# Gathered copies of queries and keys for the levels of a gated recurrence, and squares moved behind the output products

## The chip, the cores and the metric

The kernel runs on one core of a Trainium2 chip. The metric is the device time of one execution in microseconds (us); a comparison is made between medians of several executions on the same chip. The engines that matter here are TensorE (PE; its weight loads are PEld in the profile), VectorE (DVE), ScalarE (ACT) and the DMA queues of SyncE (SP) and ScalarE. GpSimd (POOL) only makes masks at the start.

## The reference

One decoder layer over 2048 positions of width 1024, in float32: a norm, a mixer with two head groups side by side, an output projection, a gated MLP with a short causal convolution, a final norm. The change lies in the first head group, four heads of a gated recurrence (key and value width 128):

```python
def hgrn2_chunkwise(q, k, v, log_f):
    """S_t = diag(f_t) S_{t-1} + k_t v_t^T,  o_t = S_t^T q_t  (k_t = 1 - f_t)."""
    ...
        b = jnp.cumsum(gi, axis=2)
        rel = b[:, :, :, None, :] - b[:, :, None, :, :]
        decay = jnp.exp(jnp.where(causal, rel, -jnp.inf))
        scores = jnp.einsum('bhtk,bhsk,bhtsk->bhts', qi, ki, decay)
        intra = jnp.einsum('bhts,bhsv->bhtv', scores, vi)
        inter = jnp.einsum('bhtk,bhkv->bhtv', qi * jnp.exp(b), state)
...
        o_hg = hgrn2_chunkwise(q_hg, k_hg, v_hg, log_f)
        o_hg = rmsnorm(o_hg, hg_norm_w[l]).reshape(B, S, HG_VAL_WIDTH)
        o_hg = (o_hg * jax.nn.silu(hg.astype(jnp.float32))).astype(h.dtype)
        ...
        mix = jnp.concatenate([o_hg, o_att], axis=-1)
        h = h + mix @ w_out[l]
```

The second head group is sliding-window attention (eight heads, four pairs `j` in the kernel).

## The kernel before, in words

The sequence is handled in two halves of 1024 positions. Each half has a mixer stage (the loop over `h` = 0 to 3, where a recurrence head and an attention pair run side by side), the output projection, and the MLP. Large matrices are multiplied as three products of high and low parts (`unit`, L212, for all projections: `f`, `hq`, `q`, `g`, and `pop` for the output projection). Features lie on the 128 partitions, positions along the free axis.

The recurrence doesn't compute decays pairwise. A chunk of 128 positions is cut by halving: at level m (1, 2, 4, ... 64), blocks of 2m positions have a left half whose keys and a right half whose queries meet. `Q` holds queries scaled by the decay from the block's start, `K` keys scaled by the decay to the block's end; `F` holds the decay over each block. At each level:

- the products of left keys and right queries go to a PSUM bank `pl` (`plev` in the profile);
- right queries are multiplied with the left block's decay (L609), left keys with the right block's (L610), and `F` is merged (L616, L620);
- the valid blocks of `pl` are put into the score tile `ST`.

How the products are formed depends on level and head. For m below 32 in heads 0 to 2 (`pairs`, `place_pairs`), ScalarE copies the left keys of two neighbouring chunks into `KK` (L566), and one product of 128 keys by 128 queries covers both chunks (L569, four products a level). Half of the result belongs to the one chunk and is copied under a mask (L585); the other half lies m partitions too low: ScalarE copies it out (`moved`, L576), a DMA on ScalarE's queue shifts it (`odd`, L579), and a masked copy places it after the next level's scaling (L588). In head 3, m below 32, each chunk has a product of its own with all 128 keys and 64 queries (L602, eight a level), and one masked copy places all (L625). Levels 32 and 64 use products of m by m in parts of the array (L607) and copies (L630).

After the levels, `K` is transposed (`pkn`, L640), states are updated (`pu`, L647; `SS`, L651), and for each of eight chunks two output products are made: scores by values (L665) and queries by state (L666), in two banks `po` of four chunks each. ScalarE squares each chunk's output right behind its products (L667) for the norm; then a root by iteration (`rsqrt`), the scaling (`on`, L674), a transpose (`pot`, L679) and the gate (L680).

The four `hg` and `at` banks of PSUM are shared out in turn: `pdiag`, `plev`, `pkn`, `pu`, `po` and `pot` all take one of two `hg` banks. The order of each engine's instructions is fixed when the program is built, by a planner that goes by its own estimates of durations and by the order in which the code names the work; `issue_after` adds that one instruction comes behind another. While head 3 runs, TensorE can fill in with the output projection, `pop`, for its first three tiles (`BEHIND` holds some of these back behind `pu`, `po` and `pot` of head 3), as far as the mixed heads exist; the tiles of attention pair 3 and of recurrence head 3 come last in the order [0, 4, 1, 5, 2, 6, 7, 3].

Of the kernel before, what the change touches and what calls it, by code (L numbers as in the profile page):

```python
# [17 lines left out]
P = 128  # L18
# [25 lines left out]
KB = 2  # L44
# [6 lines left out]
def hymba_layer(ctx: ExitStack, tc: tile.TileContext, a: dict, out: bass.AP):  # L51
# [468 lines left out]
    def hgrn(hf, h, X, invb, vs, WG, mix, p, fu=None):  # L520
# [12 lines left out]
        K = p.tile([P, HALF], F32, tag="K", name="K", bufs=1)  # L533
        nc.vector.tensor_scalar(K, f, -1.0, 1.0, op0=ALU.mult, op1=ALU.add)
        Q = p.tile([P, HALF], F32, tag="Q", name="Q", bufs=1)
# [24 lines left out]
        F, left = f, None  # L560

        def pairs():


            KK = p.tile([P, HALF // 2], F32, tag="KK", name="KK", bufs=KB)
            nc.scalar.copy(KK.rearrange("p (r b c m) -> p r c b m", r=TT // 2, c=2, m=m),  # L566
                           K.rearrange("p (r c b w m) -> p r c b w m", c=2, b=nbc, w=2, m=m)[:, :, :, :, 0])
            for r in range(TT // 2):
                marks[m] = nc.tensor.matmul(pl[:, r * P:(r + 1) * P], KK[:, r * P:(r + 1) * P],  # L569
                                            Qv[:, 2 * r * nbc:2 * (r + 1) * nbc, 1], start=True, stop=True)  # L570

        def place_pairs():

            plv = pl.rearrange("p (r c t) -> p r c t", r=TT // 2, c=2)
            moved, odd = [p.tile([P, TT // 2, 64], F32, tag="lv", name=n, bufs=LV) for n in ("moved", "odd")]
            nc.scalar.copy(moved, plv[:, :, 1])  # L576

            rows_ = P - max(m, 2)
            nc.scalar.dma_start(odd[0:rows_], moved[m:m + rows_])  # L579
            if m == 1:  # L580
                nc.scalar.dma_start(odd[rows_:rows_ + 1], moved[P - 1:P])
            STv = ST.rearrange("p (r c) (b w m) -> p r c b w m", c=2, w=2, m=m)
            mk = C.lmask[m].bitcast(U32).rearrange("p (b m) -> p b m", m=m)
            mk = mk.unsqueeze(1).to_broadcast([P, TT // 2, nbc, m])
            nc.vector.copy_predicated(STv[:, :, 0, :, 1], mk, plv[:, :, 0].rearrange("p r (b m) -> p r b m", m=m))  # L585
            r = slice(0, P - m)
            ov = odd[r].rearrange("p r (b m) -> p r b m", m=m)
            return lambda: nc.vector.copy_predicated(STv[r, :, 1, :, 1], mk[r], ov)  # L588

        for m in LEVELS:  # L590
            nb = HALF // (2 * m)
            nbc = 64 // m
            Qv = Q.rearrange("p (b w m) -> p b w m", w=2, m=m)
            Kv = K.rearrange("p (b w m) -> p b w m", w=2, m=m)
            Fv = F.rearrange("p (b w) -> p b w", w=2)
            pl = ps("hg", "plev")
            paired = m < 32 and h < HG - 1
            if paired:
                pairs()
            elif m < 32:  # L600
                for c in range(TT):
                    marks[m] = nc.tensor.matmul(pl[:, c * 64:(c + 1) * 64], K[:, c * P:(c + 1) * P],  # L602
                                                Qv[:, c * nbc:(c + 1) * nbc, 1], start=True, stop=True)
            else:
                for c in range(TT):
                    for s0 in range(0, P, 2 * m):
                        nc.tensor.matmul(pl[s0:s0 + m, c * m:(c + 1) * m], K[:, c * P + s0:c * P + s0 + m],  # L607
                                         Q[:, c * P + s0 + m:c * P + s0 + 2 * m], start=True, stop=True)
            nc.vector.tensor_tensor(Qv[:, :, 1], Qv[:, :, 1], Fv[:, :, 0:1].to_broadcast([P, nb, m]), op=ALU.mult)  # L609
            done = nc.vector.tensor_tensor(Kv[:, :, 0], Kv[:, :, 0], Fv[:, :, 1:2].to_broadcast([P, nb, m]), op=ALU.mult)  # L610
# [10 lines left out]
            if paired:  # L621
                left = place_pairs()
            elif m < 32:
                mk = C.lmask[m].bitcast(U32).rearrange("p (b m) -> p b m", m=m)
                nc.vector.copy_predicated(ST.rearrange("p c (b w m) -> p c b w m", w=2, m=m)[:, :, :, 1],  # L625
                                          mk.unsqueeze(1).to_broadcast([P, TT, nbc, m]),
                                          pl.rearrange("p (c b m) -> p c b m", c=TT, m=m))
            else:
                for s0 in range(0, P, 2 * m):
                    nc.scalar.copy(ST[s0:s0 + m, :, s0 + m:s0 + 2 * m],  # L630
                                   pl[s0:s0 + m, 0:TT * m].rearrange("p (c m) -> p c m", c=TT))
        yield
# [28 lines left out]
        for c in range(TT):  # L661
            cs = slice(c * P, (c + 1) * P)
            prev = state[:, h] if c == 0 else SS[:, c - 1]
            o = po[c // 4][:, c % 4 * P:(c % 4 + 1) * P]
            nc.tensor.matmul(o, ST[:, c], v[:, c], start=True, stop=False)  # L665
            marks["po"] = nc.tensor.matmul(o, Q[:, cs], prev, start=False, stop=True)  # L666
            nc.scalar.activation(on[:, c], o, AF.Square, accum_out=ss[:, c:c + 1])  # L667
# [626 lines left out]
```

## Time and profile before

| | |
|---|---|
| three executions | 2197.66, 2198.23, 2200.65 us (median 2198.23) |
| profiled execution, span from first to last instruction | 2198.0 us (the profile gives no other time for it) |
| mean granted TensorE clock | 0.997 |
| products on TensorE, weight loads | 11424 each |
| mixer stage, head 3 | about 342 to 407 us in the first half, 1432 to 1497 us in the second |

The profile gives, for one execution, the busy time of each engine, the chain of work that ended last, groups of instructions by line, waits, and windows of time. A product's busy time holds its way through the array, and so overlaps with the next one; how fast products really follow each other is read from the chain, where each piece counts only until the next begins.

### The profile page before, as it was taken

The page shows a single profiled execution, that of the slowest core. Times are in us where ns is not written, and L with a number is a line of the kernel's source. Part 1 is how long each engine was busy: PE and PEld are TensorE (multiplying, and loading weights), DVE is VectorE, ACT ScalarE, POOL GpSimd, SP SyncE. Part 2 cuts the span into 40 slices and gives each one's busy share as a digit, 9 for nine tenths or more (in the row PEclk, how much of TensorE's full clock was granted, in tenths as well). Part 3 has the DMA queues.
Part 4 walks back from the last instruction along what each step waited for, and adds up shares of the span by engine and source line. Part 5 has one row for each costly group of instructions (what it writes and reads, how often), then busy time and mean ns, then how long its engine had stood idle before and what let it go on. Part 6 is the DMA issues. An engine that isn't in the chain of part 4 may idle for free.

```text
span 2198.0 us, 29524 instructions
## 1 busy us (share of the span) xinstructions
PE 2180.4 (99%) x11424; PEld 1834.0 (83%) x11424; DVE 1639.5 (75%) x2451; ACT 1049.9 (48%) x1848; POOL 6.3 (0%) x28
## 2 busy tenths in 40 slices
PE   9999999999999999999999999999999999999998
PEld 7988988888888888888889889888888888888888
DVE  6567568688887888885855666677888878887766
ACT  6445544454444445335735455544644444443353
POOL 1000000000000000000000000000000000000000
PEclk9999999999999999999999999999999999999999
DMA  4101112323333234964631111114132323259643
GB/s 155 51 32 48 39 41 68 119 74 102 104 109 108 89 127 143 372 241 156 209 125 41 44 36 51 58 39 134 58 125 92 125 91 109 98 183 393 233 144 130
DMA packets 94358, 257.91 MB, mean 117 GB/s; under 512 B 11594, under 2 KB 17546, under 8 KB 94218
## 3 DMA queue, kind: packets, MB, share of 16 engines
q1 hardware_dynamic: 88992, 251.30, 33.9%
q10 hardware_dynamic: 5226, 4.73, 0.7%
q8 instruction: 89, 1.46, 0.3%
q14 instruction: 51, 0.42, 0.1%
HBM read 195.10 MB, written 57.15 MB: 115 GB/s over the span
## 4 chain that ended last, share of the span: by engine, by line
PE 95%; DVE 3%; ACT 1%; DMA 1%; issue 0%; SPq 0%; DVEq 0%; ACTq 0%
PE X L877 7%; PE X L878 7%; PE X L879 7%; PE pop L212 7%; PE hq L212 4%; PE q L212 4%; PE f L212 4%; PE g L212 4%; PE Y L879 4%; PE Y L878 4%; PE Y L877 4%; PE pdx L1088 3%; PE pdx L1089 3%; PE pdx L1090 3%; PE pdy L1089 3%; PE pdy L1088 3%
## 5 line engine op out<-in xcount | busy, mean ns | idle before, releaser
L706 ACT CAST whi<-raw 128x1024 fp32r<-128x1024 f32 x88 | 92.6, 1053 | 109.2 <-PE X L878 68.2
L877 PE MATMUL X<-T,whi 128*128 128x512 f32 x352 | 136.9, 389 | 0.0
L878 PE MATMUL X<-T,whi 128*128 128x512 f32 x352 | 136.9, 389 | 0.0
L879 PE MATMUL X<-T,wlo 128*128 128x512 f32 x352 | 136.9, 389 | 0.0
L972 DVE SCALAR_TENSOR_TENSOR y<-ga,cw,y 128x1024 f32<-128x1024 f32 x88 | 112.5, 1281 | 26.0 <-ACT y L970 26.0
L884 ACT COPY u<-X 128x512 f32<-128x512 f32 x88 | 51.4, 585 | 133.3 <-PE X L879 133.1
L707 DVE TENSOR_TENSOR wlo<-raw,whi 128x1024 fp32r<-128x1024 f32 x88 | 107.3, 1220 | 0.0
L190 ACT CAST whi<-raw 128x1024 fp32r<-128x1024 f32 x57 | 59.5, 1048 | 93.1 <-PE q L212 31.9
L707 DVE TENSOR_TENSOR xld<-raw,xhd 128x1024 fp32r<-128x1024 f32 x72 | 80.8, 1133 | 19.1 <-ACT xhd L706 18.9
L706 ACT CAST xhd<-raw 128x1024 fp32r<-128x1024 f32 x72 | 69.7, 978 | 43.6 <-DMA raw<-act0T 14.8
L212 PE MATMUL pop<-XL,whi 128*128 128x512 f32 x256 | 86.1, 396 | 2.1 <-DVE XL L224 2.1
L212 PE MATMUL pop<-XH,wlo 128*128 128x512 f32 x256 | 85.2, 393 | 0.8 <-DVE wlo L191 0.8
L212 PE MATMUL pop<-XH,whi 128*128 128x512 f32 x256 | 84.5, 397 | 0.2
L878 PEld LDWEIGHTS X<-T,whi 128*128 128x128 f32 x352 | 66.1, 188 | 13.7
L877 PEld LDWEIGHTS X<-T,whi 128*128 128x128 f32 x352 | 66.1, 188 | 13.7
L879 PEld LDWEIGHTS X<-T,wlo 128*128 128x128 f32 x352 | 66.1, 188 | 13.7
L1088 PE MATMUL pdx<-xhd,hid 128*128 128x512 f32 x192 | 74.4, 391 | 1.0 <-ACT hid L706 1.0
L1089 PE MATMUL pdx<-xld,hid 128*128 128x512 f32 x192 | 74.7, 389 | 0.0
L1090 PE MATMUL pdx<-xhd,lod 128*128 128x512 f32 x192 | 73.7, 389 | 0.0
L698 PE MATMUL pvv<-whi,XH 128*128 128x256 f32 x256 | 73.5, 288 | 0.0
L191 DVE TENSOR_TENSOR wlo<-raw,whi 128x1024 fp32r<-128x1024 f32 x57 | 69.5, 1222 | 4.2 <-ACT whi L190 4.1
L699 PE MATMUL pvv<-whi,XL 128*128 128x256 f32 x256 | 72.6, 284 | 0.0
(379 smaller groups left out, 6563.3 us busy)
## 6 DMA issues: line engine op xcount, KB each, us to landing
wr<-in_w_down SPq DMA_DIRECT2D x90, 512.0 KB, 4.8
raw<-in_w_gate SPq DMA_DIRECT2D x44, 512.0 KB, 3.6
raw<-in_w_up SPq DMA_DIRECT2D x44, 512.0 KB, 3.6
raw<-act0T SPq DMA_DIRECT2D x20, 512.0 KB, 6.1
raw<-act1T SPq DMA_DIRECT2D x20, 512.0 KB, 10.1
act0B<-y SPq DMA_DIRECT2D x33, 256.0 KB, 2.6
act1B<-y SPq DMA_DIRECT2D x33, 256.0 KB, 2.4
raw<-in_w_out SPq DMA_DIRECT2D x16, 512.0 KB, 4.7
```

Of the source, the lines that this page charges most:

```text
L212: marks["unit"] = nc.tensor.matmul(o[b], w, x[:, bs], start=f, stop=l)
L698: nc.tensor.matmul(o[:, 0:256], xh[:, t], hi[:, c], start=kt == 0, stop=False)
L699: nc.tensor.matmul(o[:, 0:256], xl[:, t], hi[:, c], start=False, stop=False)
L706: return (nc.scalar.copy(h, src), (eng or nc.vector).tensor_tensor(l, src, h.bitcast(F32), op=ALU.subtract))
L707: (eng or nc.vector).tensor_tensor(l, src, h.bitcast(F32), op=ALU.subtract))
L877: nc.tensor.matmul(o, wh[:, ws], xh, start=i == 0 and not more, stop=False, skip_group_check=more)
L878: nc.tensor.matmul(o, wh[:, ws], xl, start=False, stop=False, skip_group_check=more)
L879: r = nc.tensor.matmul(o, wl[:, ws], xh, start=False, stop=i == 3, skip_group_check=more)
L972: nc.vector.scalar_tensor_tensor(y, g[:, w:w + HALF], C.cw[:, ft, w:w + 1], y, op0=ALU.mult, op1=ALU.add)
L1088: nc.tensor.matmul(o, wh[:, i, c], ah[:, i, cols], start=f, stop=False, skip_group_check=more)
L1089: nc.tensor.matmul(o, wh[:, i, c], al[:, i, cols], start=False, stop=False, skip_group_check=more)
L1090: nc.tensor.matmul(o, wl[:, i, c], ah[:, i, cols], start=False, stop=l, skip_group_check=more)
```

## The change

- `Q` and `K` become the two halves of one tile, `QK`.
- At every level of every head ScalarE copies the right queries and the left keys, 512 elements of each, into a new tile `G` (two buffers). The column order puts chunk c beside chunk c + 4, block by block.
- The products read `G`, not `Q` and `K`. Below 32 and at 64 there are four products of 128 by 128 in every head; level 32 keeps sixteen small ones.
- Queries and keys are scaled by one DVE instruction of 2 x 512 elements.
- `place` serves every head below level 32: first half from PSUM under the mask, second half by `moved`, DMA and masked copy. Its chunk pairs are c and c + 4, and it reads `pl` with blocks of m apart. Level 64 is copied to `ST` in two parts.
- All eight squares of a head are named behind its last output product.
- The SBUF reserved for DMA descriptors is set to 256 bytes a partition.

```diff
-KB = 2
+GB = 2
...
-        K = p.tile([P, HALF], F32, tag="K", name="K", bufs=1)
+        QK = p.tile([P, 2, HALF], F32, tag="QK", name="QK", bufs=1)
+        Q, K = QK[:, 0], QK[:, 1]
         nc.vector.tensor_scalar(K, f, -1.0, 1.0, op0=ALU.mult, op1=ALU.add)
-        Q = p.tile([P, HALF], F32, tag="Q", name="Q", bufs=1)
         nc.vector.tensor_tensor(Q, q, f, op=ALU.mult)
...
+        R = TT // 2
+        def place(m, pl):
+            plv = pl.rearrange("p (r b c m) -> p r b c m", r=R, c=2, m=m)
+            moved, odd = [p.tile([P, R, 64], F32, tag="lv", name=n, bufs=LV) for n in ("moved", "odd")]
+            nc.scalar.copy(moved.rearrange("p r (b m) -> p r b m", m=m), plv[:, :, :, 1])
...
+            STv = ST.rearrange("p (c r) (b w m) -> p c r b w m", c=2, w=2, m=m)
...
+            nc.vector.copy_predicated(STv[:, 0, :, :, 1], mk, plv[:, :, :, 0])
...
+            return lambda: nc.vector.copy_predicated(STv[r, 1, :, :, 1], mk[r], ov)

         for m in LEVELS:
...
+            part, step = QK.ap[0], QK.ap[-1][0]
+            own = bass.AP(QK.tensor, QK.offset + m * step, [part, [(HALF - m) * step, 2], [2 * m * step, nb], [step, m]])
+            far = bass.AP(QK.tensor, QK.offset + m * step, [part, [(HALF - m) * step, 2], [2 * m * step, nb // 2],
+                                                           [R * P * step, 2], [step, m]])
+            G = p.tile([P, 2, HALF // 2], F32, tag="G", name="G", bufs=GB)
+            nc.scalar.copy(G.rearrange("p t (b c m) -> p t b c m", c=2, m=m), far)
             pl = ps("hg", "plev")
...
+            if m == 32:
                 for c in range(TT):
+                    for b in range(2):
+                        x = slice(c % R * P + b * 64 + c // R * m, c % R * P + b * 64 + c // R * m + m)
+                        nc.tensor.matmul(pl[2 * b * m:2 * b * m + m, c * m:(c + 1) * m], G[:, 1, x], G[:, 0, x],
+                                         start=True, stop=True)
             else:
...
+                for r in range(R):
+                    x = slice(r * P, (r + 1) * P)
+                    marks[m] = nc.tensor.matmul(pl[:, x], G[:, 1, x], G[:, 0, x], start=True, stop=True)
-            nc.vector.tensor_tensor(Qv[:, :, 1], Qv[:, :, 1], Fv[:, :, 0:1].to_broadcast([P, nb, m]), op=ALU.mult)
-            done = nc.vector.tensor_tensor(Kv[:, :, 0], Kv[:, :, 0], Fv[:, :, 1:2].to_broadcast([P, nb, m]), op=ALU.mult)
+            done = nc.vector.tensor_tensor(own, own, Fv.rearrange("p b w -> p w b").unsqueeze(3).to_broadcast([P, 2, nb, m]),
+                                           op=ALU.mult)
...
+            if m < 32:
+                left = place(m, pl)
...
+                for c in range(2):
+                    nc.scalar.copy(ST[0:m, c * R:(c + 1) * R, m:],
+                                   pl[c * m:(c + 1) * m].rearrange("p (r c m) -> p r c m", c=2, m=m)[:, :, c])
...
             marks["po"] = nc.tensor.matmul(o, Q[:, cs], prev, start=False, stop=True)
-            nc.scalar.activation(on[:, c], o, AF.Square, accum_out=ss[:, c:c + 1])
+        for c in range(TT):
+            nc.scalar.activation(on[:, c], po[c // 4][:, c % 4 * P:(c % 4 + 1) * P], AF.Square,
+                                 accum_out=ss[:, c:c + 1])
...
-    nc = bacc.Bacc("TRN2", target_bir_lowering=False, num_devices=1)
+    nc = bacc.Bacc("TRN2", target_bir_lowering=False, num_devices=1, dynamic_dma_scratch_size=256)
```

More of the change, by code (lines that the diff above doesn't have):

```diff
@@ L560, in hgrn @@
         F, left = f, None
[L562 to L576, printed above, removed]
+        R = TT // 2
[3 more added lines that the diff above has]
+            nc.scalar.copy(moved.rearrange("p r (b m) -> p r b m", m=m), plv[:, :, :, 1])
             rows_ = P - max(m, 2)
@@ L581, in place_pairs @@
                 nc.scalar.dma_start(odd[rows_:rows_ + 1], moved[P - 1:P])
[L582 removed]
+            STv = ST.rearrange("p (c r) (b w m) -> p c r b w m", c=2, w=2, m=m)
             mk = C.lmask[m].bitcast(U32).rearrange("p (b m) -> p b m", m=m)
[L584 to L585 removed]
+            mk = mk.unsqueeze(1).to_broadcast([P, R, 64 // m, m])
+            nc.vector.copy_predicated(STv[:, 0, :, :, 1], mk, plv[:, :, :, 0])
             r = slice(0, P - m)
             ov = odd[r].rearrange("p r (b m) -> p r b m", m=m)
[L588 removed]
+            return lambda: nc.vector.copy_predicated(STv[r, 1, :, :, 1], mk[r], ov)
         for m in LEVELS:
@@ L596, in hgrn @@
+            G = p.tile([P, 2, HALF // 2], F32, tag="G", name="G", bufs=GB)
+            nc.scalar.copy(G.rearrange("p t (b c m) -> p t b c m", c=2, m=m), far)
             pl = ps("hg", "plev")
[L597 to L600, printed above, removed]
+            if m == 32:
                 for c in range(TT):
-                    marks[m] = nc.tensor.matmul(pl[:, c * 64:(c + 1) * 64], K[:, c * P:(c + 1) * P],
-                                                Qv[:, c * nbc:(c + 1) * nbc, 1], start=True, stop=True)
-            else:
[L605 to L608, printed above, removed]
@@ L620, in hgrn @@
                 nc.vector.tensor_tensor(F, Fv[:, :, 0], Fv[:, :, 1], op=ALU.mult)
[L621 to L628, printed above, removed]
+            if m < 32:
+                left = place(m, pl)
+            elif m == 32:
                 for s0 in range(0, P, 2 * m):
@@ L631, in hgrn @@
                                    pl[s0:s0 + m, 0:TT * m].rearrange("p (c m) -> p c m", c=TT))
+            else:
+                for c in range(2):
+                    nc.scalar.copy(ST[0:m, c * R:(c + 1) * R, m:],
+                                   pl[c * m:(c + 1) * m].rearrange("p (r c m) -> p r c m", c=2, m=m)[:, :, c])
         yield
```

2 lines of the change are left out of this document (removed).

## The prediction, made before the changed kernel ran

> **What bounds the kernel now.** I read the busy times first, then the chain that ended last, then windows over the stages, then groups by line, and last the order of single instructions in two places. The first two rows are the busy times and the chain by engine; the others are pieces of the chain in order of time (start, length, what).
>
> ```profile
> PE 2180.4 (99%) x11424; PEld 1834.0 (83%) x11424; DVE 1639.5 (75%) x2451; ACT 1049.9 (48%) x1848; POOL 6.3 (0%) x28
> ...
> PE 95%; DVE 3%; ACT 1%; DMA 1%; issue 0%; SPq 0%; DVEq 0%; ACTq 0%
> ```
> ```profile
> 57.54 10.88 PE q L212 x48
> ```
> ```profile
> 356.55 1.75 PE plev L602 x16
> ```
> ```profile
> 173.69 0.89 PE plev L569 x8
> ...
> 200.30 1.08 PE plev L607 x16
> ```
>
> TensorE carries 95% of the chain. A "busy" PE need not be a full PE, so I check its pace: 48 products of 512 columns in 10.88 us are 0.227 us each, one after the other without a hole. Where PE is fed like that, every microsecond of TensorE work that disappears shortens the kernel, and work on the other engines is free.
>
> A rule speaks against this. The Trainium skill, page "Perfetto Trace Analysis", section "Identifying the Most-Contended Engine", says that matmul busy time is a poor measure of how near TensorE is to its limit and that the busy share of the weight loads is one of the better ones. Here that share is 83%; by that reading TensorE has room, shorter TensorE work would fall into it, and the time would stay near 2196 (rival B has the same result). The even 0.227 us speaks for PE as the bound in most of the program, but not where it starves.
>
> Where does it starve? Windows of the busy times (core 0: PE, PEld, DVE, ACT, POOL, then granted clock); last, the same stretch for the general projection line L212 alone.
>
> ```profile
> 298.00:342.00 44.00, 44.00 (x253) 36.96 (x252) 24.22 (x45) 20.27 (x41) 0.00 (x0) 1.00 0.23 73
> 342.00:407.00 65.00, 62.34 (x433) 51.91 (x432) 50.61 (x100) 25.81 (x78) 0.00 (x0) 0.97 0.16 47
> ...
> 1432.00:1497.00 65.00, 62.52 (x440) 52.42 (x439) 50.44 (x101) 26.57 (x78) 0.00 (x0) 0.97 0.16 48
> ```
> ```profile
> 351.00:364.00 13.00, 13.00 (x76) 11.33 (x76) 12.31 (x26) 8.24 (x36) 0.00 (x0) 1.00 0.17 55
> 364.00:381.00 17.00, 16.32 (x169) 13.41 (x169) 14.76 (x29) 2.48 (x5) 0.00 (x0) 0.90 0.00 1
> ```
> ```profile
> 364.00:381.00 17.00, 3.28 (x11) 1.82 (x12) 0.90 0.00 1
> ```
>
> 342 to 407 and 1432 to 1497 hold head 3 of each half. PE idles 65 - 62.34 = 2.66 and 65 - 62.52 = 2.48 us there, 5.1 together, and at a clock of 0.97 the two windows lose about 2 x 65 x 0.03 = 3.9 us more. DVE is full (12.31 of 13, 14.76 of 17), and the filling products have almost run out (11 in 17 us). So head 3 is limited by DVE's recursion, with PE nearly full beside it. In the 44 us before, DVE works 24.22: there is room, if head 3 could begin earlier.
>
> What keeps it from that? Two loops in which PE is one of the steps. Here are chain pieces around head 2's output products; then DVE and PE rows of head 1's recursion (start, length); then head 3's first products.
>
> ```profile
> 305.85 0.22 PE po L665 x2
> ...
> 310.55 0.22 PE po L666 x2
> 310.77 4.36 PE q L212 x19
> 315.13 0.22 PE po L665 x2
> ...
> 326.23 0.22 PE po L666 x2
> ```
> ```profile
> 162.51 0.69 DVE L609 TENSOR_TENSOR Q<-Q,f 128x512 f32<-128x512 f32 x1 [3.94 <-PE plev L569]
> ...
> 168.68 0.69 DVE L609 TENSOR_TENSOR Q<-Q,f 128x512 f32<-128x512 f32 x1 [0.22 <-PE plev L569]
> ```
> ```profile
> 167.57 1.07 PE L569 MATMUL plev<-Q,KK 128*128 128x128 f32 x8
> 173.52 1.05 PE L569 MATMUL plev<-Q,KK 128*128 128x128 f32 x8
> ```
> ```profile
> 344.31 1.16 PE L544 MATMUL pdiag<-hg,K 128*128 128x128 f32 x8 [0.35 <-DVE hg L680]
> ```
>
> Each time PE has to wait for another engine's answer, the fixed order puts some 19 other products in between: 4.36 us after a square (310.77 to 315.13), and 167.57 - (162.51 + 0.69) = 4.4 us from a scaling of Q to the next level's products. A level therefore takes 173.52 - 167.57 = 6 us, and eight pairs of output products, 16 x 0.22 = 3.5 us of work, take 326.45 - 305.85 = 20.6 us. Head 3's first products then wait for L680, the end of head 2.
>
> **The change part by part.** Groups by line (engine, operation, shapes, count | busy us, mean ns of one | idle before), then who waited for the squares:
>
> ```profile
> L536 DVE TENSOR_TENSOR Q<-hg,f 128x1024 f32<-128x1024 f32 x8 | 9.8, 1220 | 8.3 <-PE po L666 8.3
> L609 DVE TENSOR_TENSOR Q<-Q,f 128x512 f32<-128x512 f32 x56 | 38.6, 690 | 30.9 <-PE plev L569 18.6 <-PE plev L607 11.8 <-PE plev L602 0.4
> L625 DVE COPY_PREDICATED ST<-lmask,plev 128x512 f32<-128x512 uint32 x10 | 9.5, 949 | 0.0
> L585 DVE COPY_PREDICATED ST<-lmask,plev 128x256 f32<-128x256 uint32 x30 | 16.6, 554 | 3.4 <-ACT moved L576 3.3
> L588 DVE COPY_PREDICATED ST<-lmask,odd 126x256 f32<-126x256 uint32 x6 | 4.4, 737 | 4.1 <-DMA odd<-moved 4.1
> L588 DVE COPY_PREDICATED ST<-lmask,odd 124x256 f32<-124x256 uint32 x6 | 2.6, 442 | 7.8 <-DMA odd<-moved 7.8
> ```
> ```profile
> L706 ACT CAST whi<-raw 128x1024 fp32r<-128x1024 f32 x88 | 92.6, 1053 | 109.2 <-PE X L878 68.2 <-issue 19.1 <-PE Z L878 13.8
> L566 ACT COPY KK<-K 128x512 f32<-128x512 f32 x30 | 19.1, 636 | 29.6 <-DVE K L610 21.2 <-DVE K L534 8.2
> L706 ACT CAST T<-h 128x512 fp32r<-128x512 f32 x22 | 12.8, 617 | 3.2 <-PE pop L212 3.2
> L576 ACT COPY moved<-plev 128x256 f32<-128x256 f32 x30 | 11.1, 371 | 23.8 <-PE plev L569 23.4
> L667 ACT ACTIVATE on<-po 128x128 f32<-128x128 f32 x64 | 17.6, 275 | 58.3 <-PE po L666 56.9
> L667 ACT ACTIVATION_READ_ACCUMULATOR on<-po 128x1 f32 x64 | 12.5, 195 | 0.0
> ```
> ```profile
>   PEld po L665: 1.3, 6
> ```
> ```profile
> 1450.71 3.20 ACT sc L481 x16
> ```
>
> Chunk pairs in head 3. Levels 1 to 16 of that head now use eight products of 64 columns (L602: 16 records, 1.75 us); they become four of 128 columns, as the other heads have (L569: 8 records, 0.89). Five levels, two halves: 10 x (1.75 - 0.89) = **8.6 us less TensorE work**. Placing them costs DVE L585 and L588 where it had L625: about 2 x 0.56 against 0.95, +0.17 a level; ScalarE a copy of 0.37 and its queue one issue more (two at level 1), 12 DMAs in all. In the heads that have them DVE waits for these transfers (4.1 us over six at level 2, 7.8 over six at level 4), 0.7 to 1.3 us a level, between other work.
>
> Level 64. Eight products of 64 columns (1.08 us) become four of 128 (taken as 0.89): 8 heads x 0.19 = **1.5 us less**. Its one copy out of PSUM becomes two, about +0.15 us of ScalarE each time. Level 32 keeps sixteen small products: nothing.
>
> Gathering. Seven copies of 1024 elements a head, 56 x 1.05 = 59 us of ScalarE, replace 30 x 0.636 = 19 us; with moved and level 64 that is +45 us on an engine with 1049.9 of 2198.0. Cover: ScalarE is idle half of each window above. If the cover fails, a gather stands in order behind a block of exponentials, 3.20 us (rival C). The pattern hops: at level 1 each element comes from another place than the one before. No row has that read; KK, which strides, costs 0.636 against 0.617 for a dense one of that size, and L588 with runs of two costs 0.737 against 0.442 with runs of four. So a level-1 or level-2 gather costs between 1.05 and 1.05 x 0.737/0.442 = 1.75 us; I take 1.1, since KK is the same engine. The Trainium skill, page "SBUF — State Buffer", section "Specifications (TRN2)", says that each access that crosses to a new 16-byte line pays, unless a line is hit at least twice. KK's small excess hardly agrees, L588's does; by it the level-1 gather would stand near the upper end, 0.7 us more in each head, and in the sum that is hidden all the same.
>
> One scaling. Two of 0.69 become one of 1.22: 0.16 us less DVE a level. With the placing, head 3's DVE sum stays the same.
>
> What the scaling waits for. Before: PE's products of that level. After: only the gather, so the recursion is gather 1.05 + scaling 1.22 + two hand-overs, about 2.4 us, and PE only follows; with two G buffers and two banks, one trip of 4.4 us covers two levels, so I expect 3 us a level in place of 6: some 20 us a head.
>
> Squares last. PE no longer waits for squares of the same bank (1.3 us in all), and eight pairs can run without trips: the products end up to 16 us sooner. Against it: a square of 0.275 + 0.195 us could begin after one pair of products, 0.44 us, and now begins after the four pairs of its bank, 1.76. So in head 3, where they alternate closely, the chain may end up to 1.3 us later; I take nothing, since the later products of `pop` are there to fill PE, and keep 2.6 for the range.
>
> Q and K in one tile. K for the next head now waits for the previous head's last output product, as Q already does (L536 idles 8.3 us for it). Since that product comes sooner, cost nothing; without that, up to 1.05 us for the first gather on each head's chain.
>
> Smaller DMA scratch. It makes room for G. It changes no instruction; nothing either way.
>
> **The sum.** In heads 0 to 2 PE is full, so shorter loops give nothing by themselves; they let head 2 end and head 3 begin up to 20 us earlier, into the stretch where DVE has room, with the projections still there to fill PE. Then PE is the bound throughout and its work counts: -8.6 - 1.5 = -10.1. Of the 5.1 us idle in head 3 I take half, -2.6 (bounds: 0, and 5.1 + 3.9 for idle and clock). All else is hidden. 2198.0 - 10.1 - 2.6 = **2185.3**. The sum is made on the profiled execution, span 2198.0; I put the time around the span at nothing, since the median of the runs is 2198.23, 0.2 above.
>
> **The rivals.** B, head 3 stays bound by DVE (its DVE work is the same, and 12.31 of 13 and 14.76 of 17 us of DVE were in use). Then the 8.6 us become PE idle time, and level 64 of the other heads (6 x 0.19 = 1.1) and a microsecond of bank waits remain: about 2196. For it: DVE full from 351 to 364. Against: that is so because head 3 comes late.
>
> C, slower: gathers queue behind exponentials. Place: attention's softmax of head 3, two blocks of 3.20 us per half. If head 3 is the chain and both blocks delay a gather, 2 x 2 x 3.2 = 12.8, less 2.1 of B: about 2209. It decides once the wait passes 3.3 us a half (6.5 in all less 2.1 is 0.2%). Against: ScalarE is idle 39 of 65 us there.
>
> D, all idle time and the clock recover: 2198.0 - 10.1 - 5.1 - 3.9 = 2179. For it: head 3 earlier by 20 us, more than the PE shortage. Against: attention's own chain in head 3 doesn't shorten.
>
> **Chances.** Forecast 0.50 (2181 to 2190), B 0.22, C 0.12, D 0.16. Over 0.2% is 4.4 us, about what a measurement here can tell from no change: forecast and D are faster, 0.66; B is the same, 0.22; C slower, 0.12. To hold 8 in 10 the range takes D and B in: 2178 to 2197.
>
> **What the profile after would show.** L569-like products in head 3, 0.89 us a level, and level 64 the same; 56 gathers near 1.05 us, level 1 apart; levels some 3 us apart in heads 0 to 2; output products of a head within 5 us, not 20; head 3's first products well before 342 us; PE idle in head 3 under 3 us and a clock nearer 1.00. Wrong it would be if PE idle in head 3 grew by what its work shrank (B), or if a gather there began late behind L481 (C).

## The result, and the profile after

The changed kernel takes 2182.84 us (median of four executions, 2182.57 to 2183.7) where the kernel before takes 2197.94 on the same chip (2197.41 to 2200.65): a ratio of 0.9931, 95% interval 0.9917 to 0.9945, so 15.1 us less. Its profiled execution has a span of 2182.0 us, 16.0 under that of before. Line numbers from here on are those of the changed kernel: gather L590, products L601 (level 32: L596), scaling L602, copies of levels 32 and 64 L618 and L622, key transposes L632, output products L657 and L658.

First the busy times; then the same TensorE products before and after: all level products (`plev`) over the whole span, and the output projection (`pop`) beside head 3 and behind it (window, PE busy and count, clock, DMA share, GB/s; the first three rows are of the kernel before, the last three of the changed one).

```profile
PE 2163.2 (99%) x11280; PEld 1824.8 (84%) x11280; DVE 1629.6 (75%) x2405; ACT 1095.3 (50%) x1896; POOL 6.4 (0%) x28
```
```profile
0.00:2198.00 2198.00, 65.77 (x784) 1.00 0.35 117
...
342.00:407.00 65.00, 32.83 (x129) 0.97 0.16 47
407.00:490.00 83.00, 52.56 (x232) 1.00 0.33 110
```
```profile
0.00:2182.00 2182.00, 55.94 (x640) 1.00 0.35 119
...
322.00:390.00 68.00, 26.20 (x106) 0.97 0.24 72
390.00:490.00 100.00, 63.20 (x279) 1.00 0.32 106
```

The 16.0 us divide so. The level products need 65.77 - 55.94 = 9.8 us less. TensorE's other busy time falls by 2180.4 - 2163.2 - 9.8 = 7.4. Its idle time, span less busy, rises by 1.2 (2198.0 - 2180.4 = 17.6 to 18.8). 5.1 of the 7.4 is the unchanged `pop` (183.88 to 178.81 over the span, 768 products in both): behind head 3 a product costs 0.227 us in both kernels (52.56/232, 63.20/279); beside head 3 it cost 32.83/129 = 0.254 and now costs 0.247, and fewer of them stand there (106, not 129). These parts are rough, since the busy times of neighbouring products overlap. Counted in both traces from each product's start to the next one's, the level products give 11.2 us (55.7 to 44.5) and `pop` 4.6 (180.5 to 176.0). Part of the rest is the granted clock and not the change: the profiled execution of the kernel before has one more stretch of low clock (mean 0.66 from 1108 to 1113 us, some 1.7 us lost, on products that are the same in both).

Next, the recursion's scaling in head 2, first and last of its seven levels; the gathers of its levels 1, 2, 4 and 8 with what each waited for; and the groups of both.

```profile
233.82 1.22 DVE L602 TENSOR_TENSOR QK<-QK,f 128x1024 f32<-128x1024 f32 x1
...
251.74 1.22 DVE L602 TENSOR_TENSOR QK<-QK,f 128x1024 f32<-128x1024 f32 x1
```
```profile
221.01 1.51 ACT L590 COPY G<-QK 128x1024 f32<-128x1024 f32 x1 [3.50 <-DVE QK L536]
235.07 1.17 ACT L590 COPY G<-QK 128x1024 f32<-128x1024 f32 x1 [0.26 <-DVE QK L602]
240.12 1.05 ACT L590 COPY G<-QK 128x1024 f32<-128x1024 f32 x1 [1.67 <-DVE f L609]
243.14 1.05 ACT L590 COPY G<-QK 128x1024 f32<-128x1024 f32 x1 [1.19 <-DVE QK L602]
```
```profile
L602 DVE TENSOR_TENSOR QK<-QK,f 128x1024 f32<-128x1024 f32 x56 | 68.6, 1226 | 6.0 <-ACT G L590 5.1
L590 ACT COPY G<-QK 128x1024 f32<-128x1024 f32 x56 | 63.6, 1136 | 58.9 <-DVE QK L602 29.1 <-DVE QK L536 24.1 <-DVE f L609 3.1
```

Seven levels stand 251.74 - 233.82 = 17.9 us apart from first to last, 3.0 a level where it was 6. The scaling no longer names a product among its waits; 5.1 us for the gather are left of 30.9 us for products. The gather itself costs 1.5 us at level 1 and 1.17 at level 2, and 1.05 above.

The output products of head 2, first and last (the rows between them left out), and the span of the diagonal products and of head 3's transposes (`pdiag` begins a head, `pot` ends it; the last starts are those of head 3 in the second half).

```profile
277.70 0.38 PE L657 MATMUL po<-v,ST 128*128 128x128 f32 x2
...
281.99 0.38 PE L658 MATMUL po<-SS,QK 128*128 128x128 f32 x2
```
```profile
L544 PE MATMUL pdiag<-hg,QK x128: 270/275/275, 68.2 to 1405.9; 128*128 128x128 f32 x128
...
L673 PE MATMUL pot<-ident,on x64: 270/272/329, 130.6 to 1467.7; 128*128 128x128 f32 x64
```

They take 4.7 us, not 20.6. Head 3 of the second half begins at 1405.9, where it began at 1434.8; some 8 of these 29 us are the first half's own gain.

Last, head 3: windows with the 24 us in front of it; then the rows of ScalarE and TensorE around a new wait, in both halves.

```profile
298.00:322.00 24.00, 24.00 (x129) 19.44 (x128) 9.62 (x13) 6.16 (x7) 0.00 (x0) 1.00 0.15 45
322.00:390.00 68.00, 64.18 (x427) 54.71 (x426) 55.54 (x103) 43.42 (x105) 0.00 (x0) 0.97 0.24 72
...
1405.00:1470.00 65.00, 61.93 (x420) 53.56 (x419) 54.42 (x102) 42.46 (x105) 0.00 (x0) 0.97 0.24 75
```
```profile
361.56 0.40 ACT L481 ACTIVATE sc<-sc,m 128x128 f32<-128x128 f32 x1 [0.55 <-DVE m L477]
...
365.04 0.74 ACT L622 COPY ST<-plev 64x256 f32<-64x256 f32 x2
```
```profile
365.83 1.11 PE L632 MATMUL pkn<-ident,QK 128*128 128x128 f32 x4 [2.86 <-ACT ST L622]
...
1446.36 0.66 PE L632 MATMUL pkn<-ident,QK 128*128 128x128 f32 x4 [2.44 <-ACT ST L622]
```

TensorE still idles there: 68 - 64.18 = 3.8 us and 65 - 61.93 = 3.1, and the granted clock is 0.97 as before. 5.3 of these 6.9 us are one wait, twice: the second bank of key transposes needs the PSUM bank that holds the level-64 products; L622 empties it, and stands on ScalarE behind attention's block of exponentials, 361.56 to 364.8.

The clock of 0.97 is a mean. It is full in most of head 3 and low in one stretch of each half, behind this wait (columns as in the windows above):

```profile
362.00:366.00 4.00, 1.14 (x8) 0.91 (x9) 1.19 (x4) 3.94 (x19) 0.00 (x0) 0.94 0.00 0
366.00:370.00 4.00, 4.00 (x24) 3.83 (x25) 3.25 (x5) 1.25 (x3) 0.00 (x0) 0.63 0.00 0
370.00:374.00 4.00, 3.42 (x39) 2.62 (x38) 3.89 (x13) 1.55 (x8) 0.00 (x0) 1.00 0.00 0
```

By this the stretch loses some 4 x 0.06 + 4 x 0.37 = 1.7 us, an estimate. The kernel before has one such stretch in each half too. In its second half, eight `pop` products stood 0.427 us apart there, from 1439.8 to 1443.3, so some of the slow `pop` is clock, which now falls on other products.

### The profile page after: what moved, and what is told of

Same layout as the page of the kernel before. It is cut to its first block, busy times and chain, and to the rows that moved or that the text cites. A ratio compares the mean times of both kernels' runs of the same rounds, so it can differ in the third digit from the quotient of the medians.

```text
span 2182.0 us, 29301 instructions
## 1 busy us (share of the span) xinstructions
PE 2163.2 (99%) x11280; PEld 1824.8 (84%) x11280; DVE 1629.6 (75%) x2405; ACT 1095.3 (50%) x1896; POOL 6.4 (0%) x28
## 5 line engine op out<-in xcount | busy, mean ns | idle before, releaser
L590 ACT COPY G<-QK 128x1024 f32<-128x1024 f32 x56 | 63.6, 1136 | 58.9 <-DVE QK L602 29.1
```

## The experiments

Medians in us; ratio to the kernel before on the same chip, with its 95% interval; then the clock loss (below); then from the profiled execution the span less PE busy, and where head 3 of the second half begins and ends (last starts of `pdiag` and `pot`).

| kernel | median | ratio | clock loss | PE idle | head 3 |
|---|---|---|---|---|---|
| before | 2197.9 | | 3.5 | 17.6 | 1434.8 to 1487.0 |
| changed | 2182.8 | 0.9931 [0.9917, 0.9945] | 4.4 | 18.8 | 1405.9 to 1467.7 |
| e1 | 2198.2 | 0.9999 [0.999, 1.0008] | 5.0 | 25.4 | 1430.4 to 1481.6 |
| e2 | 2202.3 | 1.0021 [1.0012, 1.0029] | 7.4 | 24.7 | 1415.9 to 1488.6 |
| e3 | 2195.5 | 0.9989 [0.998, 0.9998] | 8.4 | 23.1 | 1412.3 to 1481.7 |
| e4 | 2192.1 | 0.997 [0.9958, 0.9981] | 4.4 | 20.8 | 1410.2 to 1477.3 |
| e5 | 2182.7 | 0.9931 [0.9918, 0.9943] | 4.8 | 20.5 | 1405.6 to 1468.3 |
| e6 | 2206.6 | 1.0039 [1.0025, 1.0052] | 7.5 | 29.4 | 1424.2 to 1492.9 |
| e7 | 2190.8 | 0.9967 [0.9955, 0.998] | 5.7 | 22.9 | 1410.5 to 1476.7 |
| e8 | 2194.1 | 0.9982 [0.9973, 0.999] | 9.2 | 24.9 | 1412.3 to 1481.0 |
| e9 | 2179.6 | 0.9911 [0.9897, 0.9924] | 1.6 | 18.2 | 1403.0 to 1462.6 |
| e10 | 2181.1 | 0.9918 [0.9904, 0.9931] | 2.6 | 18.1 | 1405.2 to 1465.1 |
| e11 | 2178.7 | 0.9909 [0.9896, 0.9923] | 3.3 | 16.7 | 1403.2 to 1463.6 |
| e12 | 2180.4 | 0.9918 [0.9905, 0.9932] | 2.6 | 17.1 | 1404.3 to 1464.6 |

The clock loss is an estimate: for every execution on record, span x (1 - mean granted clock), and the mean of these. The clock is listed to 0.001, which is 2.2 us of one execution, so a mean is good to about half a us. The kernel before shows what it is worth: its executions at 0.997 took 2201.3 us on average (4 of 61), those at 0.999 took 2197.7 (26 of 61). In e2, e3, e6 and e8 the loss is 3 to 5 us above that of the kernel each is made from, in e9 to e12 it is 1 to 3 below. In the profiled executions most stretches of low clock follow a wait of TensorE, but not every wait has one (e1's of 2.59 us has none), and what sets them was not tested.

Two cautions. The spans of profiled executions lie up to 2.8 us under their kernel's median and e1's 5.5, so rows of different kernels are compared for what waits on what, not for a few us of span; and the kernel before had medians from 2197.7 to 2199.2 in the four groups of runs, so the ratio is the better measure of small differences. And the planner orders every kernel anew: e5, e9, e10 and e11 keep the order of the changed kernel's TensorE products almost everywhere, the other runs less, and e6 least, so a difference of 2 or 3 us in those can be the plan's.

The first four runs set three theories against each other: T1, TensorE's saved work counts only once head 3 begins earlier, so both halves of the change are needed; T2, TensorE is the bound anyway and its work counts by itself; T3, the loops without TensorE give the gain.

**e1: chunk pairs in head 3 alone** (the kernel before, with the smaller DMA scratch).

```diff
-            paired = m < 32 and h < HG - 1
+            paired = m < 32
```

> The kernel before, with chunk pairs in head 3 as in the other heads (TensorE work of its levels 8.6 us less), and nothing else of the change. Theory 1 (both parts are needed: shorter TensorE work counts only once head 3 begins earlier, since head 3 is otherwise limited by VectorE's recursion): 2194 to 2198 us, TensorE idle in head 3 grows by about what its work shrinks. Theory 2 (TensorE is the bound anyway): 8.6 us less, 2189. Theory 3 (the gain comes from the loops without TensorE alone): no change, 2198.

2198.2: nothing, although the 8.6 us of products are gone. TensorE waits instead; the row is its longest wait in head 3, for the low part of the projection's input.

```profile
1436.00 0.74 PE L212 MATMUL pop<-XL,whi 128*128 128x512 f32 x2 [2.59 <-DVE XL L224]
```

T2 falls. TensorE's idle time grew by 7.8 us. This is what rival B of the prediction had described, and for this part alone it holds.

**e2: squares behind the products alone** (the kernel before).

```diff
-            nc.scalar.activation(on[:, c], o, AF.Square, accum_out=ss[:, c:c + 1])
+        for c in range(TT):
+            nc.scalar.activation(on[:, c], po[c // 4][:, c % 4 * P:(c % 4 + 1) * P], AF.Square,
+                                 accum_out=ss[:, c:c + 1])
```

> The kernel before, with all squares of a head behind its last output product, and nothing else. Theory 1: the output products of heads 0 to 2 run within 5 us in place of 20, so head 3 begins up to 15 us earlier and fills better: 2 to 4 us less, 2194 to 2196. Theory 2: only TensorE's waits for a square's bank go, about 1 us: 2197. Theory 3: if the output products are the loop that mattered most, most of the 15 us: 2185 to 2190.

2202.3, by the ratio some 4 us more than before: slower, which no theory had. The larger clock loss (7.4 against 3.5) is about as much as the whole difference. Head 3 begins 19 us sooner (1415.9) and ends 1.6 later. Its first scaling comes only 17 us after the head's first products (324.6 to 341.6 in the first half), from the first scaling to the last it takes 33.6 us (28.3 before), and TensorE waits late in the head; two such waits in each half, here those of the second:

```profile
1460.61 0.40 PE L506 MATMUL poT<-po,V 128*64 128x128 f32 x2 [1.19 <-DVE m L474]
...
1467.22 0.73 PE L212 MATMUL pop<-XH,whi 128*128 128x512 f32 x2 [2.76 <-ACT XH L516]
```

An earlier begin of head 3's products is worth nothing here, where its recursion still waits for TensorE level by level.

**e3: both together**, the kernel before with e1's and e2's edits.

> The kernel before, with chunk pairs in head 3 and the squares last, without the gathered copies (and with the small DMA scratch). Theory 1: the squares let head 3 begin earlier and a part of the 8.6 us counts: 2188 to 2193. Theory 2: 8.6 and 1 us less, 2188. Theory 3 (gathering is what brought the gain): 2195 to 2198.

2195.5, by the ratio some 2 us less than before: T1's form of "both are needed" is too weak. From here to the changed kernel is the gather (with the one scaling, and level 64 for 1.5 us): 2195.5 - 2182.8 = 12.7 us, most of the whole (up to 4.0 of it the difference in clock loss).

**e4: the changed kernel with the TensorE work put back.** Head 3's products below level 32 are cut in halves of 64 queries.

```diff
+                    n = 64 if m < 32 and h == HG - 1 else P
+                    for s in range(r * P, (r + 1) * P, n):
-                    marks[m] = nc.tensor.matmul(pl[:, x], G[:, 1, x], G[:, 0, x], start=True, stop=True)
+                        marks[m] = nc.tensor.matmul(pl[:, s:s + n], G[:, 1, x], G[:, 0, s:s + n], start=True, stop=True)
```

> The changed kernel, with head 3's products below level 32 cut into halves of 64 queries, eight a level, so that TensorE's work there is again 1.75 us a level and all else stays. The result is the same. Theories 1 and 2: 8.6 us more, 2191 to 2192. Theory 3 (TensorE has room in head 3, the loops decide): 2183 to 2185.

2192.1: 9.3 us more (8.5 by the ratios), at the same clock loss, for 64.50 - 55.94 = 8.6 us more of level products (e4's whole-span sum is 64.50). The same work that e1 removed for nothing now has its full price. So T1 stands in this form: with the gather, TensorE's work in head 3 counts.

**e5: the new wait taken away.** Level 64's copies by VectorE in head 3.

```diff
-                    nc.scalar.copy(ST[0:m, c * R:(c + 1) * R, m:],
+                    (nc.vector.tensor_copy if h == HG - 1 else nc.scalar.copy)(ST[0:m, c * R:(c + 1) * R, m:],
```

> The changed kernel, with head 3's two copies of the level-64 products out of PSUM given to VectorE, so that they no longer stand behind a 3.2 us block of exponentials on ScalarE. Theory W (that wait is what holds PE for 3.02 and 2.60 us ahead of the second bank of key transposes, and nothing stands behind it): both stalls go and the time falls by 4 to 6 us, to 2177 to 2179. Rival (head 3 is held by VectorE's recursion or by attention's own chain; the wait is only where the shortage shows): the idle time of TensorE moves to other products of head 3 and the time stays at 2181 to 2184.

2182.7, no change. The wait for L622 is gone and others hold what it held: the state updates wait for the copies of the transposed keys, attention's transposes for the scaled exponentials.

```profile
366.74 2.05 PE L639 MATMUL pu<-v,Kn 128*128 128x128 f32 x16 [2.03 <-ACT Kn L633]
370.72 0.41 PE L506 MATMUL poT<-po,V 128*64 128x128 f32 x2 [1.05 <-DVE pp L498]
...
1447.41 0.68 PE L495 MATMUL ppt<-ident,sc 128*128 128x128 f32 x4 [3.48 <-DVE sc L486]
```

The rival holds: the largest wait in the profile was where a shortage showed, not what caused it.

**e6: the loop through TensorE put back.** Gather, shapes and scaling stay; the products of levels 1 to 16 and 64 read the queries where the scaling writes them.

```diff
-                    marks[m] = nc.tensor.matmul(pl[:, x], G[:, 1, x], G[:, 0, x], start=True, stop=True)
+                    q_far = bass.AP(QK.tensor, QK.offset + (r * P + m) * step,
+                                    [part, [2 * m * step, nbc], [R * P * step, 2], [step, m]])
+                    marks[m] = nc.tensor.matmul(pl[:, x], G[:, 1, x], q_far, start=True, stop=True)
```

> The changed kernel, but the products of levels 1 to 16 and 64 read their queries from the place where the scaling writes them (same shapes, same gather of both), so that the scaling waits for TensorE's products again, as before the change. Theory L (the shorter TensorE work counts only since the recursion no longer waits for TensorE): levels 5 to 6 us apart again, head 3's first products at 335 us or later, and 2191 to 2196. Rival P (the shorter work and the single scaling are the gain, the loop is not): 2182 to 2185.

2206.6: 23.8 us over the changed kernel and 8.5 over the kernel before, beyond Theory L's range. In groups: the scaling (L604 here) and the products (L603); then two scalings of head 1.

```profile
L604 DVE TENSOR_TENSOR QK<-QK,f 128x1024 f32<-128x1024 f32 x56 | 68.4, 1222 | 93.4 <-PE plev L603 89.7 <-ACT G L590 3.2
...
L603 PE MATMUL plev<-QK,G 128*128 128x128 f32 x384 | 56.5, 292 | 5.0 <-ACT G L590 5.0
```
```profile
180.69 1.21 DVE L604 TENSOR_TENSOR QK<-QK,f 128x1024 f32<-128x1024 f32 x1
188.51 1.23 DVE L604 TENSOR_TENSOR QK<-QK,f 128x1024 f32<-128x1024 f32 x1
```

VectorE waits 89.7 us for TensorE. These two scalings are 7.8 us apart; from first to last it is 6.9 a level in head 1 and 6.2 in head 2, where the changed kernel has 3.5 and 3.0: the trip of about 4.4 us through TensorE's order, and now the gather in front of it. The products also took 292 ns each on average in place of 275 and 61.71 us in all in place of 55.94, and the clock loss is 3.1 us larger, so up to 9 of the 24 us are not the loop's directly. The 15 that are left are as much as the whole gain: it is the copy of the queries, which no product needs for its shape, that makes the change pay.

**e7: squares back between the products**, in the changed kernel (e2's edit undone).

> The changed kernel with the squares back between the output products. Theory L: output products take 15 to 20 us of a head again, head 3 begins some 10 us later than after the change, and a part of the gain is lost, 2185 to 2190. Rival S (squares behind the products cost head 3's chain as much as they give the other heads, as the kernel before with this part alone suggests, 4 us slower): the same or faster, 2179 to 2184.

2190.8, 8.0 us more, a little over Theory L's range; head 3 begins 4.6 us later and ends 9.0 later. The same edit that cost some 4 us on the kernel before (e2) and gave 2.7 on top of the pairs (e3 against e1) gives 8.0 here.

**e8: every gather twice.**

```diff
             nc.scalar.copy(G.rearrange("p t (b c m) -> p t b c m", c=2, m=m), far)
+            nc.scalar.copy(G.rearrange("p t (b c m) -> p t b c m", c=2, m=m), far)
```

> The changed kernel with each gather done twice into the same place: 56 more copies of about 1.1 us on ScalarE, each ahead of a level's products and scaling. Theory H (the gather is hidden behind other work, in head 3 too): 2182 to 2186. Rival G (in head 3 the gather is on the path that sets the end): 14 more copies of 1.1 us, up to 15 us, 2190 to 2198. If it were on the path in all heads, 62 us: 2245.

2194.1, 11.3 us more: not hidden. 63 us of ScalarE work were added, 14/56 of it, 16 us, in head 3; 11.3 is near that share and far from 63. But up to 4.8 of the 11.3 us are clock loss (9.2 against 4.4). The scaling's group (L603 here):

```profile
L603 DVE TENSOR_TENSOR QK<-QK,f 128x1024 f32<-128x1024 f32 x56 | 68.6, 1225 | 23.8 <-ACT G L591 23.6
```

VectorE's waits for the gather rise from 5.1 to 23.6 us; 6.4 of these stand in head 3 of the two halves, where the changed kernel has none. That the 11.3 us are head 3's share is not shown beyond this.

**e9 and e10: shorter exponentials beside head 3**; e10 has e5's edit too. Both leave out the softmax's maximum and sum for each chunk of queries in attention's last group.

```diff
-                    nc.scalar.activation(sc[:, kv, i], sc[:, kv, i], AF.Exp, bias=m[:, kv, i:i + 1],
-                                         accum_out=den[:, kv, i:i + 1])
+                    nc.scalar.activation(sc[:, kv], sc[:, kv], AF.Exp, bias=m[:, kv, 0:1], accum_out=d[:, kv])
```

> The changed kernel, with the exponentials of the attention group beside head 3 in 2 instructions of 512 elements a block in place of 8 pairs of 128 (one maximum and one sum for four queries' chunks: this part of the softmax is left out). A block takes about 1.4 us of ScalarE in place of 3.2; four such blocks in the kernel. Theory A (head 3 ends when attention's chain of copies, softmax and products ends): 4 x 1.8 = 7 us less, 2175 to 2179. Rival R (head 3's recursion is the chain; attention only shows where TensorE has run out of other work): at most the part that stands in front of the level-64 copies, 0 to 3.6 us less, 2179.5 to 2183.

> The shortened exponentials and the level-64 copies on VectorE together. Theory A: as with the exponentials alone, and the last wait of the recursion gone too: 2173 to 2178. Rival R: 2180 to 2183, as with either alone. If the two are in parallel and end within 3 us of each other, each alone gives little and both together 5 us or more.

2179.6 and 2181.1: 3.2 and 1.8 us less than the changed kernel, for 6.4 us less ScalarE work in e9 (busy 1095.3 to 1088.9). Both lie in rival R's ranges, the first at their lower edge. By the ratios it is 4.4 and 2.9 us, which puts e9 beyond R's 3.6 and at the edge of theory A, so e9 alone doesn't decide. Most of it can be clock: the loss is 2.7 and 1.8 us smaller, and e9's profiled execution has a clock of 1.00 all through head 3. As both together give no more than the shorter exponentials alone, the two waits are not two parallel chains of which each covers the other.

**e11: keys gathered by GpSimd in head 3.**

```diff
+                for t, e in enumerate((nc.scalar.copy, nc.gpsimd.tensor_copy)):
+                    src = bass.AP(QK.tensor, far.offset + t * (HALF - m) * step, [far.ap[0]] + list(far.ap[2:]))
+                    e(G[:, t].rearrange("p (b c m) -> p b c m", c=2, m=m), src)
```

> The changed kernel, with head 3's gather shared: queries by ScalarE (512 elements), keys by GpSimd, which does nothing else there. Theory G (head 3's gathers are on the path that sets the end; a second copy of each cost 11 us): 14 gathers of about 0.6 us in place of 1.1, 4 to 6 us less, 2177 to 2179, if GpSimd needs no more than 0.7 us for its half. If GpSimd needs 1.5 us or more, the price is 14 times the excess over 1.1: slower than after the change, 2188 or more. Rival Q (the second copy cost its time because ScalarE's queue is full at the head's begin, not because a level waits for its gather): 2181 to 2184 at any GpSimd time up to 1.1 us.

2178.7: the best of all, 4.1 us under the changed kernel; its executions (2177.91 to 2182.33) all lie below those of the change. Theory G had the number, but the rows don't show its mechanism. Head 3's scalings, first and last of the first half (L607 here), and ScalarE's first exponential:

```profile
326.14 1.22 DVE L607 TENSOR_TENSOR QK<-QK,f 128x1024 f32<-128x1024 f32 x1
...
362.13 1.22 DVE L607 TENSOR_TENSOR QK<-QK,f 128x1024 f32<-128x1024 f32 x1
```
```profile
357.32 0.42 ACT L481 ACTIVATE sc<-sc,m 128x128 f32<-128x128 f32 x1
```

From first to last they take 36.0 us; in the changed kernel it is 33.9 (326.28 to 360.14). What moved is the block of exponentials, which begins at 357.32, 4.2 us sooner, ahead of the gather of level 64. Head 3 also has a clock of 1.00 in this profiled execution, and the clock loss is 1.1 us smaller on average. Relief of ScalarE fits the gain, and so do another order of ScalarE's instructions from the planner and the clock; the runs don't tell them apart.

**e12: the same in all four heads** (the condition on `h` left out).

> The gather shared between ScalarE and GpSimd in every head, not in head 3 alone. Theory E (heads 0 to 2 matter because they set when head 3 begins): their levels shorten by some 0.4 us each, head 3's first products come 3 to 8 us sooner than with head 3's share alone, and 2173 to 2177. Rival F (TensorE is full in heads 0 to 2 and head 3 now begins early enough; only its own levels still count): 2177.5 to 2181, as with head 3 alone.

2180.4, rival F: no better than head 3's share alone, and head 3 begins no sooner (1404.3 against 1403.2).

## Why the prediction came out right, and where its steps were wrong

It said 2185.3 by -10.1 of TensorE work and -2.6 of idle time; 15.1 us were gained. That the sum came within 2.5 us is in part luck: parts that it put at nothing are large and of both signs (8.0 us for the squares in e7, up to 11.3 for a second gather in e8). The time around the span, also put at nothing, is 1.7 us in the changed kernel's profiled execution (2183.7 against 2182.0).

- **TensorE's work, -10.1.** Right in size (9.8 busy, 11.2 from start to start) and in its condition, that it counts once head 3's chain is shorter: e4 prices head 3's 8.6 us at 9.3 with the gather, e1 at nothing without. The rule from the Trainium skill, page "Perfetto Trace Analysis", section "Identifying the Most-Contended Engine", judges TensorE's headroom by the weight-load share rather than by matmul busy time. The prediction's reading of it, that 83% leaves room, fits e1 and not e4. That share is 83% and 84% in these two, so here it doesn't tell whether shorter TensorE work pays; which wait ends last does.
- **Two loops through TensorE, 6 us a level to 3.** Right: 3.0 us in head 2, 3.5 in head 1 ((178.54 - 157.39)/6), and e6 shows that it is the loop. But the reason given for its worth was incomplete. The prediction had the loops pay by an earlier begin of head 3. e2 begins 19 us earlier and loses. Nor did head 3's own levels become shorter: from the first scaling to the last they take 33.9 us, where they took 28.3. The rows after those of head 1 are head 3's first and last scalings in the first half: the kernel before, the changed one, e2 and e6. Head 3's first products start at 322.8, 324.6 and 326.9 us in the last three, but only in the changed kernel does its first scaling follow in 3.5 us; in e2 and e6, with the loop through TensorE, it takes 17 (9 in the kernel before, which begins at 342.8). By these rows what counts is when the recursion begins: it ends 20 us sooner than before (30 in the second half, 1470.3 to 1440.3).

```profile
157.39 1.22 DVE L602 TENSOR_TENSOR QK<-QK,f 128x1024 f32<-128x1024 f32 x1
...
178.54 1.20 DVE L602 TENSOR_TENSOR QK<-QK,f 128x1024 f32<-128x1024 f32 x1
```
```profile
351.95 0.69 DVE L609 TENSOR_TENSOR Q<-Q,f 128x512 f32<-128x512 f32 x1
...
380.22 0.68 DVE L609 TENSOR_TENSOR Q<-Q,f 128x512 f32<-128x512 f32 x1
```
```profile
326.28 1.22 DVE L602 TENSOR_TENSOR QK<-QK,f 128x1024 f32<-128x1024 f32 x1
...
360.14 1.22 DVE L602 TENSOR_TENSOR QK<-QK,f 128x1024 f32<-128x1024 f32 x1
```
```profile
341.61 0.69 DVE L609 TENSOR_TENSOR Q<-Q,f 128x512 f32<-128x512 f32 x1
...
375.19 0.69 DVE L609 TENSOR_TENSOR Q<-Q,f 128x512 f32<-128x512 f32 x1 [1.26 <-PE plev L607]
```
```profile
343.98 1.22 DVE L604 TENSOR_TENSOR QK<-QK,f 128x1024 f32<-128x1024 f32 x1
...
378.22 1.23 DVE L604 TENSOR_TENSOR QK<-QK,f 128x1024 f32<-128x1024 f32 x1 [2.33 <-PE plev L603]
```

- **Idle time, -2.6.** The term that was mis-sized. Span less PE busy rose by 1.2 in place of falling, the clock in head 3 stayed at 0.97, and "PE idle in head 3 under 3 us" failed (3.8 and 3.1). What came instead was 7.4 us less busy time on other products, most of it `pop`, and a part of it clock. The net of the two is -6.2 where -2.6 was taken (-4.9 from start to start). Head 3's loss sat less in TensorE's idle time than in slow products that count as busy; the pace of fed products, 0.227 us, was measured for the first claim and not held against the products beside head 3.
- **Gathers hidden.** Wrong for a second set: e8 gives 11.3 us, up to 4.8 of it clock. What the first set costs no run shows. The cover named was that ScalarE is idle half of each window; but head 3's new begin falls among casts and copies of the projection's input, and ScalarE is busy for 43.4 of 68 us there.
- **Gather of 1.1 us at levels 1 and 2.** 1.51 and 1.17. The Trainium skill, page "SBUF — State Buffer", section "Specifications (TRN2)", had an access pay for each new 16-byte line unless a line is hit twice: level 1, which hops at every element, pays 0.46 us over 1.05, level 2, with two neighbours, 0.12. The trace agrees with the rule more than with the choice made, at level 1. At level 2, where every line is hit twice, the rule has no price and the trace has 0.12; and L588 with runs of two, which the prediction took as agreeing, pays (0.737 against 0.442) where the rule would not.
- **Squares last, nothing taken.** Wrong by its interaction: 8.0 us as part of the change (e7), a loss of some 4 alone (e2), nearly all of which can be clock.
- **Rival C's place.** A copy did get behind the 3.20 us exponentials, the level-64 one and not a gather, 2.86 and 2.44 us of TensorE's time. By e5 it cost nothing in the end.
- **One tile for Q and K; the scratch.** The keys' instruction shows no idle time before it in the changed kernel, as assumed. The scratch was in e1 and not tried alone; e1's zero leaves it no large effect unless another cancelled it.

What holds head 3's last 4 us of idle time stays open: removing the largest wait (e5), shortening the softmax (e9) and relieving ScalarE (e11) give 0, 3.2 and 4.1 us, of which up to 2.7 and 1.1 us in the last two are clock.

## What to carry to other kernels

When a recursion on one engine and a fixed order of products on a full TensorE share a buffer, try copying what the products read: here a copy of 1 us that lets the recursion begin and run on was worth more than the products that the same change saved. A part that is worth nothing alone (e1) or costs (e2) can be needed for the whole; try parts in the changed kernel, by taking one out, as well as in the old one. And a large wait in front of a TensorE product is worth removing only if nothing stands close behind it. Before a difference of 2 to 5 us is given a cause, compare the granted clock of all executions of both kernels: here the clock could make up all of e2's loss and most of e9's gain.

## What the runs showed that was not expected

TensorE pays for hops too. In e6, where the products read their queries in place, the products of level 1 (queries hop at every element) took some 336 ns each (a record's own time, which overlaps the next one's), those of level 2 283 and of level 4 275; the rows are the eight records of each of these levels in head 1 as one stretch, 1.49, 1.12 and 1.05 us. It is the same order as the gather's 1.51, 1.17 and 1.05 on ScalarE, and with 8 heads some 8 x (0.44 + 0.07) = 4 of the 6 us by which e6's products were longer.

```profile
163.42 1.49 PE L603 MATMUL plev<-QK,G 128*128 128x128 f32 x8
172.02 1.12 PE L603 MATMUL plev<-QK,G 128*128 128x128 f32 x8
179.20 1.05 PE L603 MATMUL plev<-QK,G 128*128 128x128 f32 x8
```

In e11 GpSimd's half of a gather (512 elements) took 0.61 to 2.32 us, ScalarE's half, by the same pattern, 0.60 to 0.86 (columns: shortest, median and longest in ns). Hops don't explain GpSimd's longest: 2.30 and 2.32 us are level 4, with runs of four, while level 1 took 0.85 in the first half. Why is open.

```profile
L595 POOL COPY G<-QK x14: 613/656/2317, 304.2 to 1437.7; 128x512 f32<-128x512 f32 x14
L595 ACT COPY G<-QK x14: 603/622/856, 315.3 to 1437.5; 128x512 f32<-128x512 f32 x14
```
